# LayerNorm inverse roots moved to GpSimd, and the last two chunks of the last LayerNorm reordered

## Chip, core and metric

The kernel runs on one core of one Trainium2 chip. The metric is the device time of one execution in microseconds (us), the median of three runs. TensorE (PE) multiplies, VectorE (DVE), ScalarE (ACT) and GpSimd (POOL) do the element-wise work, and SyncE (SP) issues most of the transfers. DVE and ACT can read the matmul accumulators (PSUM, tiles `mm` and `ax`); POOL is only used on SBUF tiles here.

## The reference

One decoder layer over 1024 prompt tokens and 32 sample tokens, width 1024. What matters here are its three LayerNorms over the width:

```python
def layer_norm(x, g, b):
    mu = mean(x); var = mean((x - mu) ** 2)
    return (x - mu) * rsqrt(var + 1e-5) * g + b

h = layer_norm(ALPHA * x + 0.5 * swiglu(x, f1...), ln1_g, ln1_b)     # LN1
...  # z = h @ w_in, attention, gated MLP branch, mix
h = layer_norm(ALPHA * h + mix, ln2_g, ln2_b)                         # LN2
y = layer_norm(ALPHA * h + 0.5 * swiglu(h, f2...), ln3_g, ln3_b)      # LN3, the output
```

## The kernel before

Data lie transposed: features over the 128 partitions, the 1056 tokens along the free axis, in four chunks of 264 tokens (`C = 264`, `NC = 4`). A chunk of the residual stream is two tiles `Y[0]`, `Y[1]` of 128 x 4 x 264, four feature blocks each (`KH = 4`). Every LayerNorm is done chunk by chunk while TensorE goes on with the blocks of the next chunk:

- `block` (L925 in the two feed-forward networks, L1711 before LN2) adds a matmul result to `Y`; `square_step` squares it on ACT (L594) and sums the squares on DVE (L598, and L585 to L591 for the last blocks). `center` subtracts the mean (L549 on TensorE, L555 on DVE).
- `norm(c, i, mode)` is a generator, one per chunk `c` and LayerNorm `i`. It sums the squares over the partitions by a matmul with a column of ones (L607, result 128 x 3 in PSUM), takes the inverse root of variance plus epsilon on that 128 x 3 tile (names `X`), spreads the root to all partitions by a matmul with the identity (L621, result 128 x 264 in PSUM), multiplies `Y` by it on DVE (L632, one instruction of 128 x 1056 for each half `j`), applies gain and bias on ACT (L640; in the last chunk half of them on DVE, L637), and stores (L646 in LN3).
- The root has two forms before: `rsqrt` (L664 to L668: a Sqrt on ACT, which needs its own activation table, then a reciprocal and a Newton step of three instructions on DVE) and `rsqrt_dve` (L655 to L660: an integer first guess and three Newton steps, 11 DVE instructions).

The order of the work is set in two steps. The code emits the steps of the generators between matmul blocks (`tick`; `HOP` says how many steps a root may take before its spreading matmul is emitted), and a list scheduler then places each instruction in its engine's queue; work marked urgent (`high_priority`) goes ahead. Each engine then runs its own queue strictly in order, and waits at an instruction whose operands are not ready. What the chunks `NC - 2` and `NC - 1` (the last but one and the last, called chunk 2 and chunk 3 below; the first are chunk 0 and chunk 1) do in LN3 is the end of the program. Weights are split on the way in and out of LN1 and LN2 into a rounded part (ACT, L253) and a rest (DVE, L254), so ACT and DVE are busy there with other work too. An L338 or L348 on DVE prepares sums of normalized chunks for the next matrix product.

Of the kernel before, what the change touches and what calls it, by code (L numbers as in the profile page):

```python
# [14 lines left out]
I32 = mybir.dt.int32  # L15
AF = mybir.ActivationFunctionType
ALU = mybir.AluOpType
# [4 lines left out]
P = 128  # L22
# [5 lines left out]
C = 264  # L28
NC = NT // C
KH = KB // 2  # L30
# [14 lines left out]
EPL = EPS / ALPHA**2  # L45
# [11 lines left out]
URGENT = 300  # L57
# [7 lines left out]
HOP = (4, 1, 4)  # L65
WARM = 2
MAGIC = float(0x5F3759DF)
# [16 lines left out]
class Trunk:  # L84
# [392 lines left out]
    def spill_sums(self, i, a, b):  # L477

        nc = self.nc
        x11, x12, x21, x22 = a[:, :, 0], a[:, :, 1], b[:, :, 0], b[:, :, 1]  # L480

        def out(p, t):
            hi = self.M([P, 2, C], F32R)
            self.split(hi, t.bitcast(F32R), t)
            dst = self.sums[i, ORDER.index(p)]
            nc.sync.dma_start(dst[:, 0], hi.bitcast(F32))
            nc.sync.dma_start(dst[:, 1], t)
            return self.pause(GAP)

        sub = lambda t, u, v: nc.vector.tensor_tensor(t, u, v, op=ALU.subtract)  # L490
        t1, t2 = (self.M([P, 2, C]) for _ in range(2))
        sub(t1, x12, x11)
        yield from out(1, x11)
        sub(t2, x22, t1)
        yield from out(5, t1)
        sub(x12, x22, x12)
        yield from out(7, x12)
        t4 = self.M([P, 2, C])
        sub(t4, x21, t2)
        yield from out(6, t2)  # L500
        yield from out(3, x22)
        yield from out(4, t4)
        yield from out(2, x21)
# [96 lines left out]
    def norm(self, c, i, mode, Y, s):  # L600
        nc = self.nc
        offs = (0, P, C - P)
        if mode != "out" or c < NC - 1:
            nc.vector.tensor_tensor(s[:, 0], s[:, 0], s[:, 1], op=ALU.add)
        pv = self.ax_tile()[:, :3]
        for j, o in enumerate(offs):
            nc.tensor.matmul(pv[:, j : j + 1], s[:, 0, o : o + P], self.ones[:, 0:1], start=True, stop=True)  # L607
        rt = self.X([P, 2, 3], "rs")
        r, t = rt[:, 0], rt[:, 1]
        if c == NC - 1 and i == 1 or c == NC - 2 and mode == "out":  # L610
            self.rsqrt_dve(r, t, self.X([P, 3], "rx", 1), pv, EPL)
        else:
            self.rsqrt(r, t, pv, EPL)
        if i == 1 and c == NC - 2:
            nc.scalar.activation(self.X([P, 2], "warm", 1)[:, :1], r[:, :1], AF.Silu)
        for _ in range(HOP[i]):
            yield
        pb = self.ax_tile()[:, :C]
        for j, o in enumerate(offs):
            lo = 0 if j < 2 else 2 * P - o  # L620
            nc.tensor.matmul(  # L621
                pb[:, o + lo : o + P], r[:, j : j + 1].to_broadcast([P, P]), self.ident[:, lo:], start=True, stop=True
            )
        yield
        while mode == "out" and c == NC - 2 and NC - 1 not in self.lns:
            yield
        if mode != "out":
            A = self.normed[c]
        cast = None
        for j in range(2):  # L630
            y = Y[j]
            nc.vector.tensor_tensor(y, y, pb.unsqueeze(1).to_broadcast([P, KH, C]), op=ALU.mult)  # L632
            for m in range(KH):
                n = KH * j + m
                g, b = self.vec(2 * i, n), self.vec(2 * i + 1, n)
                if c == NC - 1 and m % 2:
                    nc.vector.tensor_scalar(y[:, m], y[:, m], g, b, op0=ALU.mult, op1=ALU.add)  # L637
                else:
                    with self.tc.issue_after(cast) if cast else ExitStack():
                        nc.scalar.activation(y[:, m], y[:, m], AF.Identity, bias=b, scale=g)  # L640
            yield
            if mode == "out":
                parts = 2 if c == NC - 1 else 1
                for m in range(parts):
                    e = slice(m * KH // parts, (m + 1) * KH // parts)
                    nc.sync.dma_start(self.a["yo"][c, j][:, e], y[:, e])  # L646
            else:
                cast = self.split(*A[j], y)[0]
                nc.sync.dma_start(self.hD[i][c, j], y)
            yield  # L650

    def rsqrt_dve(self, r, t, x, v, eps):
        nc = self.nc
        tt = nc.vector.scalar_tensor_tensor
        nc.vector.tensor_scalar(x, v, eps, None, op0=ALU.add)  # L655
        nc.vector.tensor_scalar(r.bitcast(I32), x.bitcast(I32), -0.5, MAGIC, op0=ALU.mult, op1=ALU.add)
        for _ in range(3):
            nc.vector.tensor_tensor(t, x, r, op=ALU.mult)
            tt(t, t, -0.5, r, op0=ALU.mult, op1=ALU.mult)
            self.chain = tt(r, t, 1.5, r, op0=ALU.add, op1=ALU.mult).ins  # L660

    def rsqrt(self, r, t, v, eps):
        tt = self.nc.vector.scalar_tensor_tensor
        self.nc.scalar.activation(r, v, AF.Sqrt, bias=self.eps[eps])  # L664
        self.nc.vector.reciprocal(r, r)
        tt(t, v, eps, r, op0=ALU.add, op1=ALU.mult)
        tt(t, t, -0.5, r, op0=ALU.mult, op1=ALU.mult)
        self.chain = tt(r, t, 1.5, r, op0=ALU.add, op1=ALU.mult).ins  # L668
# [156 lines left out]
    def out(self, w2, i, mode, ready, between, load):  # L825
        nc = self.nc
# [44 lines left out]
        for g in range(NG):  # L871
            for np in range(KB // 2):
                final = g == NG - 1 and np == KB // 2 - 1
# [53 lines left out]
        for c in range(NC):  # L927
# [15 lines left out]
                self.tick(STEPS["out"])  # L943
            self.start_ln(c, i, mode)
        if mode == "out":
            self.drain()

    def tables(self):
# [960 lines left out]
```

## Time and profile before

| | |
|---|---|
| runs | 2154.41 us median of 3 (2153.32 to 2157.72) |
| profiled execution | 2154.51 us, of which the span of the profile is 2152.5 us |
| granted TensorE clock | 0.994 of full speed |
| busy | PE 2122.6 us, DVE 1549.5 us, ACT 889.4 us, POOL 317.1 us |
| roots, four in each LayerNorm | 10 with `rsqrt` (L664), 2 with `rsqrt_dve` (chunk 3 of LN2, chunk 2 of LN3) |
| table loads of ACT for L664 | 4, of 1283 ns each |
| LN1, LN2, LN3 in the trace | first L607 at 679.2, 1401.4 and 2105.0 us |

"Busy" is summed over instructions of one engine; an engine is idle when the instruction at the head of its queue waits. A row of the timeline gives start, duration, engine, line, operation, tiles, and in brackets the idle time before it and who ended it. Times are us from the start of the span.

### The profile page before, as it was taken

What the parts mean: (1) busy time and instruction counts of PE and PEld (TensorE: products, weight loads), DVE (VectorE), ACT (ScalarE), POOL (GpSimd) and SP (SyncE); (2) the same over time, 40 slices, a digit from 0 to 9 for tenths busy, and PEclk for the clock granted to TensorE, in tenths of its full rate; (3) what the DMA queues carried; (4) which work ended last, traced back from release to release, by engine and by line L of the source; (5) the groups of instructions that cost most, each with busy time, mean ns of one, the idle gap of its engine ahead of it and who ended that gap; (6) DMA issues with size and microseconds to landing.
All of it is one profiled execution on the core that took longest, in us unless ns stands there. A gap on an engine that the chain in (4) does not pass through costs nothing.

```text
span 2152.5 us, 43254 instructions
## 1 busy us (share of the span) xinstructions
PE 2122.6 (99%) x17307; PEld 2085.6 (97%) x17307; DVE 1549.5 (72%) x2727; ACT 889.4 (41%) x1680; POOL 317.1 (15%) x249
## 2 busy tenths in 40 slices
PE   9999999999999999999999999999999999999997
PEld 8999999999999999999988889999999999999997
DVE  8877767747789834777767758787667777657887
ACT  5444444422124634333476544164444444421224
POOL 0432322200000011323000000000323323100000
PEclk9999999999999999999999999999999999999998
DMA  4444555598885335676865765423454554596852
GB/s 155 145 140 170 183 166 168 189 338 315 327 325 176 130 103 177 201 231 198 296 211 187 223 190 177 154 110 110 144 174 156 183 173 153 194 408 267 311 186 81
DMA packets 168377, 426.51 MB, mean 198 GB/s; under 512 B 24352, under 2 KB 59792, under 8 KB 165488
## 3 DMA queue, kind: packets, MB, share of 16 engines
q1 hardware_dynamic: 167744, 423.21, 56.4%
q8 instruction: 135, 2.21, 0.4%
q10 hardware_dynamic: 432, 0.54, 0.1%
q14 instruction: 66, 0.54, 0.1%
HBM read 304.31 MB, written 165.57 MB: 218 GB/s over the span
## 4 chain that ended last, share of the span: by engine, by line
PE 89%; DVE 4%; DMA 4%; POOL 1%; issue 1%; ACT 0%; SPq 0%; ACTq 0%; DVEq 0%; POOLq 0%
PE ax L242 46%; PE mm L242 39%; DMA R<-wz 1%; PE ax L1206 1%; DMA M<-kv 1%; DMA S<-cD 1%; PE ax L1255 1%; PE ax L1232 1%; DVE W L254 1%; DMA S<-hD 0%; DVE S L632 0%; POOL Q L392 0%; POOL Q L387 0%; DVE S L254 0%; PE ax L621 0%
## 5 line engine op out<-in xcount | busy, mean ns | idle before, releaser
L242 PE MATMUL mm<-S,W 128*128 128x264 f32 x5400 | 713.6, 287 | 8.0 <-ACT S L253 2.3
L242 PE MATMUL ax<-S,W 128*128 128x264 f32 x5400 | 708.6, 285 | 1.3 <-ACT S L1034 1.1
L242 PEld LDWEIGHTS mm<-S,W 128*128 128x128 f32 x5400 | 677.1, 189 | 21.0 <-issue 7.0
L242 PEld LDWEIGHTS ax<-S,W 128*128 128x128 f32 x5400 | 678.5, 189 | 4.0 <-ACT S L1034 2.4
L242 PE MATMUL ax<-S,S 128*128 128x264 f32 x3240 | 475.9, 284 | 1.0 <-ACT S L1034 0.5
L242 PEld LDWEIGHTS ax<-S,S 128*128 128x128 f32 x3240 | 427.7, 188 | 1.7 <-DVE S L1043 0.9
L242 PE MATMUL mm<-S,S 128*128 128x264 f32 x2280 | 359.4, 286 | 2.6 <-DVE S L925 2.6
L242 PEld LDWEIGHTS mm<-S,S 128*128 128x128 f32 x2280 | 311.0, 189 | 3.9 <-issue 2.9
L253 ACT CAST W<-R 128x256 fp32r<-128x256 f32 (+2 forms) x175 | 130.6, 764 | 307.5 <-PE mm L242 139.9
L386 POOL TENSOR_TENSOR Q<-R 128x512 f32<-128x512 f32 x49 | 68.1, 1390 | 800.8 <-DMA R<-w13a 198.2
L254 DVE TENSOR_TENSOR W<-R,W 128x256 fp32r<-128x256 f32 (+2 forms) x175 | 154.6, 887 | 23.3 <-ACT W L253 21.7
L253 ACT CAST W<-Q 128x1024 fp32r<-128x1024 f32 (+1 forms) x78 | 76.8, 984 | 217.2 <-POOL Q L387 88.1
L820 DVE SCALAR_TENSOR_TENSOR S<-ax,S 128x264 f32<-128x264 f32 x240 | 99.7, 429 | 66.1 <-PE ax L242 65.7
L462 DVE TENSOR_TENSOR S<-ax,M 128x264 f32<-128x264 f32 x82 | 32.6, 433 | 144.7 <-PE ax L242 144.7
L254 DVE TENSOR_TENSOR S<-Q,S 128x1024 fp32r<-128x1024 f32 (+1 forms) x78 | 113.6, 1456 | 5.5 <-ACT S L253 5.4
L110 POOL CAST S<-ones 128x1 fp32r<-128x1 f32 x36 | 12.5, 355 | 675.7 <-PE ax L242 226.0
L254 DVE TENSOR_TENSOR W<-Q,W 128x1024 fp32r<-128x1024 f32 (+1 forms) x78 | 90.6, 1161 | 29.6 <-ACT W L253 29.6
L253 ACT CAST S<-Q 128x1024 fp32r<-128x1024 f32 (+1 forms) x78 | 76.7, 984 | 68.4 <-PE ax L242 49.8
L254 DVE TENSOR_TENSOR S<-S,M 128x528 fp32r<-128x528 f32 x72 | 84.6, 1175 | 2.5 <-ACT M L253 0.7
L253 ACT CAST S<-R 128x512 fp32r<-128x512 f32 (+1 forms) x62 | 42.0, 677 | 98.9 <-DMA sumsA<-S 40.6
L387 POOL TENSOR_TENSOR Q<-Q,R 128x512 f32<-128x512 f32 x49 | 81.0, 1653 | 2.7
L394 POOL TENSOR_TENSOR Q<-R,Q 128x512 f32<-128x512 f32 x49 | 79.7, 1627 | 1.2
(209 smaller groups left out, 2042.5 us busy)
## 6 DMA issues: line engine op xcount, KB each, us to landing
ws<-st SPq DMA_DIRECT2D x144, 256.0 KB
S<-sumsA SPq DMA_DIRECT2D x63, 528.0 KB
S<-sumsB SPq DMA_DIRECT2D x63, 528.0 KB
M<-kv SPq DMA_DIRECT2D x96, 256.0 KB
sumsA<-M SPq DMA_DIRECT2D x90, 264.0 KB
sumsB<-M SPq DMA_DIRECT2D x90, 264.0 KB
R<-w13b SPq DMA_DIRECT2D x44, 512.0 KB
R<-w13a SPq DMA_DIRECT2D x42, 512.0 KB
```

The lines of the kernel that those rows point to most:

```text
L110: self.nc.gpsimd.tensor_copy(t[:, 0, :1] if len(shape) == 3 else t[:, :1], self.ones[:, :1])
L242: mm = lambda a, b, s, e: nc.tensor.matmul(o, a[:, cc], b, start=s, stop=e, skip_group_check=True)
L253: a = self.nc.scalar.copy(hi, src)
L254: b = self.nc.vector.tensor_tensor(lo, src, hi.bitcast(F32), op=ALU.subtract)
L386: tt(s12[:, lo], cd[:, lo], cd[:, hi], op=ALU.add)
L387: tt(s12[:, hi], s12[:, lo], ab[:, lo], op=ALU.subtract)
L394: tt(s34[:, hi], ab[:, hi], s12[:, hi], op=ALU.subtract)
L462: go(one, 5, False, lambda x: tt(h[:, x, 1], one[x], p7[:, x], op=ALU.add))
L820: nc.vector.scalar_tensor_tensor(y(x, r, e), bank[x], HALF, y(x, r, e), op0=ALU.mult, op1=ALU.add)
L1206: m = nc.tensor.matmul(pS[h][:, r, :nk], q[e, i * P : (i + 1) * P], k[e, k0 : k0 + nk], start=True, stop=True)
L1232: nc.tensor.transpose(pT[r][:, h, o], s[:, r, h, o], self.ident)
L1255: nc.tensor.matmul(pv[0][e, (i % 4) * P : (i % 4 + 1) * P], V[:, i - (nb - 1) + b, e], sT[:, r, h, b * P : b * P + P], start=b == 0, stop= ...
```

## The change

Eleven of the twelve roots (all four of LN1, all four of LN2 and three of the four of LN3) now use the new `rsqrt_pool`: an ACT instruction copies variance plus epsilon from PSUM to SBUF (Identity, no table of its own), and 13 POOL instructions on 128 x 3 elements follow, each reading what the one before wrote. Only chunk 3 of LN3 keeps `rsqrt` with its Sqrt. In LN3 chunk 2 four things are new: a small Sqrt on ACT that loads the table ahead of time (L617 in the new numbering), one step instead of four between the root and its spreading matmul, the scaling L632 in quarters (128 x 528), of which the last two are placed behind the root of chunk 3, and that root's first step is emitted urgently before the rest. The last of the four transfers of chunk 3 is issued by ACT's queue instead of SP's.

```diff
-        if c == NC - 1 and i == 1 or c == NC - 2 and mode == "out":
-            self.rsqrt_dve(r, t, self.X([P, 3], "rx", 1), pv, EPL)
+        if c == NC - 1 and mode == "out":
+            self.rsqrt(r, t, pv, EPL)
         else:
-            self.rsqrt(r, t, pv, EPL)
+            self.rsqrt_pool(r, t, self.X([P, 3], "rx"), pv, EPL)
         if i == 1 and c == NC - 2:
             nc.scalar.activation(self.X([P, 2], "warm", 1)[:, :1], r[:, :1], AF.Silu)
-        for _ in range(HOP[i]):
+        if mode == "out" and c == NC - 2:
+            nc.scalar.activation(self.X([P, 2], "warm", 1)[:, :1], self.eps[EPL], AF.Sqrt)
+        for _ in range(1 if mode == "out" and c == NC - 2 else HOP[i]):
             yield
...
-            nc.vector.tensor_tensor(y, y, pb.unsqueeze(1).to_broadcast([P, KH, C]), op=ALU.mult)
+            parts = 2 if mode == "out" and c == NC - 2 else 1
+            for x in range(0, KH, KH // parts):
+                e = y[:, x : x + KH // parts]
+                with self.chained() if parts > 1 and j else ExitStack():
+                    nc.vector.tensor_tensor(e, e, pb.unsqueeze(1).to_broadcast([P, KH // parts, C]), op=ALU.mult)
...
-                    nc.sync.dma_start(self.a["yo"][c, j][:, e], y[:, e])
+                    queue = nc.scalar if j and m else nc.sync
+                    queue.dma_start(self.a["yo"][c, j][:, e], y[:, e])
...
+    def rsqrt_pool(self, r, t, x, v, eps):
+        tt, ts = self.nc.gpsimd.tensor_tensor, self.nc.gpsimd.tensor_scalar
+        self.nc.scalar.activation(x, v, AF.Identity, bias=self.eps[eps])
+        ts(r.bitcast(I32), x.bitcast(I32), -0.5, MAGIC, op0=ALU.mult, op1=ALU.add)
+        for _ in range(3):
+            tt(t, x, r, op=ALU.mult)
+            tt(t, t, r, op=ALU.mult)
+            ts(t, t, -0.5, 1.5, op0=ALU.mult, op1=ALU.add)
+            tt(r, r, t, op=ALU.mult)
...
         if mode == "out":
+            final = self.bg.pop()
+            with self.tc.high_priority(offset=URGENT):
+                next(final)
+            self.bg.append(final)
             self.drain()
```

Over the whole program POOL gets 143 instructions more, DVE 56 fewer; ACT loses five table loads (four for L664 and one behind them) and gets one (L617), two more copies, and one transfer to issue. Outside the three LayerNorms all queues are the same.

TensorE's queue in LN1, at the spreading matmul of chunk 0 (`ax_8169` before, `ax_8179` after; `mm_8329` and `mm_8267` are block results, twelve L242 each; L549 is the mean of chunk 3). Before:

```order
L242 MATMUL mm_8329<-S_7823,W_7869 128x264
L242 MATMUL mm_8329<-S_7822,W_7870 128x264
L621 MATMUL ax_8169<-ident,X_8126 128x128 x2
L621 MATMUL ax_8169<-ident,X_8126 128x8
L549 MATMUL ax_8178<-M_8134,ones 128x264
```

After:

```order
L242 MATMUL mm_8267<-S_7823,S_7994 128x264
L242 MATMUL mm_8267<-S_7822,S_7995 128x264
L623 MATMUL ax_8179<-ident,X_8126 128x128 x2
L623 MATMUL ax_8179<-ident,X_8126 128x8
L549 MATMUL ax_8188<-M_8144,ones 128x264
```

The spreading matmul (L621, now L623) has moved two blocks ahead: 36 L242 stand between chunk 0's L607 and it, where there were 60.

DVE's queue at the end of the program, from the last sum of squares of chunk 3 (L591) on; `ax_25672` and `ax_25739` are chunk 2's spread root, `ax_25771` and `ax_25857` chunk 3's variance, `ax_25781` and `ax_25881` chunk 3's spread root. Before:

```order
L591 TENSOR_TENSOR M_25621<-M_25621,M_25756 128x264
L660 SCALAR_TENSOR_TENSOR X_25628<-X_25628 128x3
L632 TENSOR_TENSOR S_22648<-S_22648,ax_25672 128x1056
L632 TENSOR_TENSOR S_22874<-S_22874,ax_25672 128x1056
L665 RECIPROCAL X_25775<-X_25775 128x3
L666 SCALAR_TENSOR_TENSOR X_25775<-ax_25771,X_25775 128x3
L667 SCALAR_TENSOR_TENSOR X_25775<-X_25775 128x3
L668 SCALAR_TENSOR_TENSOR X_25775<-X_25775 128x3
L632 TENSOR_TENSOR S_22768<-S_22768,ax_25781 128x1056
```

After:

```order
L591 TENSOR_TENSOR M_25714<-M_25714,M_25854 128x264
L638 TENSOR_TENSOR S_22721<-S_22721,ax_25739 128x528 x2
L682 RECIPROCAL X_25861<-X_25861 128x3
L683 SCALAR_TENSOR_TENSOR X_25861<-ax_25857,X_25861 128x3
L684 SCALAR_TENSOR_TENSOR X_25861<-X_25861 128x3
L685 SCALAR_TENSOR_TENSOR X_25861<-X_25861 128x3
L638 TENSOR_TENSOR S_22947<-S_22947,ax_25739 128x528 x2
L638 TENSOR_TENSOR S_22841<-S_22841,ax_25881 128x1056
```

Half of chunk 2's scaling (L632, now L638) has moved behind chunk 3's root.

ACT's queue at the same place. Before:

```order
L585 ACTIVATE M_25738<-S_22876 128x264
L664 ACTIVATE X_25775<-ax_25771,eps_165 128x3
L640 ACTIVATE S_22648<-S_22648,cols 128x264 x4
L640 ACTIVATE S_22874<-S_22874,cols 128x264 x4
L640 ACTIVATE S_22768<-S_22768,cols 128x264 x2
L640 ACTIVATE S_22876<-S_22876,cols 128x264 x2
```

After:

```order
L585 ACTIVATE M_25836<-S_22949 128x264
L646 ACTIVATE S_22721<-S_22721,cols 128x264 x2
L681 ACTIVATE X_25861<-ax_25857,eps_165 128x3
L646 ACTIVATE S_22721<-S_22721,cols 128x264 x2
L646 ACTIVATE S_22947<-S_22947,cols 128x264 x4
L646 ACTIVATE S_22841<-S_22841,cols 128x264 x2
L646 ACTIVATE S_22949<-S_22949,cols 128x264 x2
L653 DMA yo<-S_22949 128x528
```

The Sqrt of chunk 3 (L664, now L681) now stands behind two gain-and-bias instructions of chunk 2, and the last transfer stands at the end of this queue.

## The prediction

> **What bounds the kernel now.** I read the page's head first, then the waits of TensorE, then the timeline of the end and of each LayerNorm.
>
> ```profile
> span 2152.5 us, 43254 instructions
> PE 2122.6 (99%) x17307; PEld 2085.6 (97%) x17307; DVE 1549.5 (72%) x2727; ACT 889.4 (41%) x1680; POOL 317.1 (15%) x249
> ...
> PE mm L242 <- DVE S L925: 3.2, 4, 1.9
> PE ax L621 <- DVE X L668: 2.7, 1, 2.7
> ...
> PE ax L621 <- DVE X L660: 1.6, 1, 1.6
> ```
>
> TensorE is busy for 99% of the span. A wait row gives the total, how often, and the longest. The spreading matmul L621 waited for a root only twice, 2.7 and 1.6 us, and both times at the end of the program. So ten of the twelve roots are already hidden: there the change can only lose, and only if a root comes later than TensorE reaches L621. What it can win lies in the end, whose rows follow (start, duration, engine, line, operation, and in brackets the idle time before it).
>
> ```profile
> 2133.43 0.72 PE L607 MATMUL ax<-ones,M 128*128 128x1 f32 x6
> ...
> 2138.42 0.43 DVE L591 TENSOR_TENSOR M<-M,M 128x264 f32<-128x264 f32 x1
> 2138.77 0.15 DVE L660 SCALAR_TENSOR_TENSOR X<-X 128x3 f32<-128x3 f32 x1
> 2139.07 0.81 PE L621 MATMUL ax<-ident,X 128*128 128x128 f32 x6 [1.64 <-DVE X L660]
> 2139.73 0.81 PE L607 MATMUL ax<-ones,M 128*128 128x1 f32 x6
> 2139.91 2.42 DVE L632 TENSOR_TENSOR S<-S,ax 128x1056 f32<-128x1056 f32 x2 [0.99 <-PE ax L621]
> 2140.58 0.26 ACT L664 ACTIVATE X<-ax,eps 128x3 f32<-128x3 f32 x1 [3.47 <-PE ax L607]
> 2141.20 4.09 ACT L640 ACTIVATE S<-S,cols 128x264 f32<-128x264 f32 x8 [0.36 <-DVE S L632]
> 2142.25 0.17 DVE L665 RECIPROCAL X<-X 128x3 f32<-128x3 f32 x1
> 2143.22 1.42 PE L621 MATMUL ax<-ident,X 128*128 128x128 f32 x6 [2.69 <-DVE X L668]
> 2144.68 2.42 DVE L632 TENSOR_TENSOR S<-S,ax 128x1056 f32<-128x1056 f32 x2 [1.60 <-PE ax L621]
> 2147.02 1.39 DVE L637 TENSOR_SCALAR S<-S,cols 128x264 f32<-128x264 f32 x4
> 2148.89 0.40 SPq L646 DMA_DIRECT2D yo<-S  x1
> ...
> 2148.50:2149.00 0.50, 0.00 (x0) 0.00 (x0) 0.00 (x0) 0.00 (x0) 0.00 (x0) 0.50 1.03 397
> ```
>
> Chunk 3's Sqrt (L664) has its value by 2140.84, but DVE is in chunk 2's two L632 until 2142.33, and the reciprocal only starts at 2142.25. This 1.4 us lies on the path that ends the program: reciprocal, Newton step, L621, L632, gain and bias, transfer.
>
> **The price of a root on GpSimd.** The first row below is the list of line L110 (minimum, median and maximum in ns), the last but two its mean; the trace has no 128 x 3 arithmetic on POOL.
>
> ```profile
> L110 POOL CAST S<-ones x36: 178/184/1268, 597.3 to 2041.7; 128x1 fp32r<-128x1 f32 x36
> 1517.17 1.29 POOL L387 TENSOR_TENSOR Q<-Q,R 128x512 f32<-128x512 f32 x1
> 1518.55 1.29 POOL L394 TENSOR_TENSOR Q<-R,Q 128x512 f32<-128x512 f32 x1
> L110 POOL CAST S<-ones 128x1 fp32r<-128x1 f32 x36 | 12.5, 355 | 675.7 <-PE ax L242 226.0 <-DMA S<-sumsA 188.7 <-DVE S L1692 96.7
> ...
> 708.66 1.23 DVE L254 TENSOR_TENSOR S<-R,S 128x1024 fp32r<-128x1024 f32 x1 [1.25 <-PE mm L242]
> 708.81 1.12 POOL L110 CAST S<-ones 128x1 fp32r<-128x1 f32 x1 [54.62 <-PE mm L242]
> ```
>
> A tiny POOL instruction takes 0.184 us, and one that needs the result of the one before it (L394 reads what L387 wrote) starts 0.09 us after its end. I take 0.184 + 0.08 = 0.264 us for each of the 13 steps: 3.4 us undisturbed. From above, the mean of the casts, 0.355, gives 13 x 0.435 = 5.65 us. Between these ends I stay at the median and count the disturbance by itself: the cast of 708.81 took 1.12 instead of 0.18 us, and it ended 0.04 us after the DVE instruction with two SBUF operands (L254) that had begun 0.15 us before it. So a step that meets such a DVE instruction waits for its end. The 0.355 is the same effect, averaged over 36 places.
>
> [...]
>
> [...]
>
> **LN1 and LN2, where the spreading matmul has moved.** What counts for a root is how many L242 stand between its L607 and its spreading matmul. In the order of the changed kernel these are, for chunks 0 to 3: LN1 36, 51, 60, 51 (before 60, 67, 107, 42); LN2 51, 51, 65, 67 (before 30, 39, 42, 66); LN3 48, 67 for chunks 0 and 1 (before 55, 45). The tight one is chunk 0 of LN1:
>
> ```profile
> 679.20 0.72 PE L607 MATMUL ax<-ones,M 128*128 128x1 f32 x6
> 679.42 1.05 ACT L253 CAST W<-R 128x1024 fp32r<-128x1024 f32 x1 [2.49 <-DMA R<-wzp]
> 680.16 4.62 PE L242 MATMUL mm<-S,S 128*128 128x264 f32 x36 [0.23 <-DVE S L925]
> 680.49 1.28 ACT L664 ACT_TABLE_LOAD   x1
> 681.05 1.22 DVE L254 TENSOR_TENSOR W<-R,W 128x1024 fp32r<-128x1024 f32 x1
> 681.78 0.26 ACT L664 ACTIVATE X<-ax,eps 128x3 f32<-128x3 f32 x1
> 682.26 0.41 DVE L546 TENSOR_TENSOR M<-M,S 128x264 f32<-128x264 f32 x1
> 682.70 0.71 DVE L598 TENSOR_TENSOR M<-M,M 128x528 f32<-128x528 f32 x1
> 684.28 0.71 DVE L598 TENSOR_TENSOR M<-M,M 128x528 f32<-128x528 f32 x1
> 684.62 3.09 PE L242 MATMUL mm<-S,W 128*128 128x264 f32 x24
> 687.54 0.73 PE L621 MATMUL ax<-ident,X 128*128 128x128 f32 x6
> ```
>
> The first 36 L242 take 684.62 - 680.16 = 4.46 us, 0.124 us each. With only these ahead of it TensorE is at the spreading matmul at 684.62 instead of 687.54. The root: the table load is gone, so the Identity runs right behind the cast, to about 680.75; 3.4 us of POOL steps end at 684.2 if nothing meets them. The four DVE instructions with two SBUF inputs in that stretch are 1.22 + 0.41 + 0.71 + 0.71 = 3.05 us; a POOL step that waits loses the rest of one, and I take two thirds, 2.0 us. The root is ready at 686.2, TensorE waits 1.6 us (0 to 3). Behind the root on DVE stand the two scalings (2.42 us, as in the row of 2139.91), and behind them the evictions of the next blocks, which come late too: another 0 to 2.4, I take 0.7. Together +2.3 us.
>
> Chunk 2 of LN2 has a second way to be late: the warm Silu on ACT (L615) reads the root, so ACT stands at it until POOL's chain is done, with the rounding of a weight behind it in its queue.
>
> ```profile
> 1437.74 0.73 PE L607 MATMUL ax<-ones,M 128*128 128x1 f32 x6
> 1438.33 5.39 PE L242 MATMUL mm<-S,W 128*128 128x264 f32 x42
> 1440.91 1.25 DVE L338 TENSOR_TENSOR S<-S,S 128x1056 f32<-128x1056 f32 x1
> 1442.28 1.22 DVE L254 TENSOR_TENSOR W<-R,W 128x1024 fp32r<-128x1024 f32 x1
> ```
>
> 65 matmuls are 8.1 us, so TensorE is there at about 1446.5. In these 8 us some seven DVE instructions like L338 and L254 (1.25 and 1.22 us) run, so a chain of 3.4 us that waits for two to five of them takes 6 to 9.6 us and is late by 0 to 1.9; I take 1.0. Chunk 3 of LN2 (67 matmuls, 8.3 us, but with POOL in place of DVE) 0 to 1.5, I take 0.4. The four roots with 48 or 51 matmuls in LN1 and LN2 and chunk 0 of LN3 have 6.0 to 6.3 us. They need some 0.5 us to the end of the Identity plus a chain which, with waits as in chunk 0 of LN1, is 5.4 us: 5.9. They are in time by 0.1 to 0.4, and I add 0.3 us for them together. The removed table loads (1.28 us each) and the 56 DVE instructions removed are worth nothing by themselves: no wait of TensorE there names ACT's root, and both engines have idle time to spare (41% and 72% busy). LN1 to LN3 without the end: +4.0 us, from 0 to +9.
>
> **The end.** Chunk 2's L607 now stands 11 matmuls earlier (37 behind it, 26 before), 1.4 us, so it ends at about 2132.8, with the Identity at 2133.1 and the chain of 3.4 us plus 0.7 to 1.1 of waits done at 2137.2 to 2137.6. Its L621 can then run once the last L242 is done, at some 2137.7, and not at 2139.07. Chunk 3's L607 hangs on L591, which ended at 2138.85 with chunk 2's root steps on DVE (L660 and those before it) between; without them it can be a little earlier, but I take the same time. DVE then does two quarters of chunk 2 (1.21 us) before the L607 of chunk 3 is answered. ACT does two gain-and-bias instructions (4.09 / 8 = 0.51 each) and the Sqrt (0.26) behind them, ending about 2140.8, as before. The reciprocal, which waited until 2142.25 for the second L632, can start at 2140.8: -1.45 us. The other two quarters (1.21 us) fit into DVE's wait of 1.60 us for the last L621, and everything from there on keeps its lengths. If POOL's chain for chunk 2 is 2 us longer, the quarters begin later and nothing is won; so -1.8 to 0, I take -1.45.
>
> The last transfer on ACT's queue is worth 0: the issue on SP at 2148.89 is the last of a row of issues, and in the window from 2148.50 on the DMA engines are 100% busy (1.03) at 397 GB/s. Transfers wait for the DMA engines there, not for a queue. The small Sqrt for the table costs nothing, ACT idled 3.47 us ahead of L664.
>
> **The sum.** The profiled execution took 2154.51 us (span 2152.5 and 2.0 around it), 0.1 above the median of 2154.41. 2154.5 + 4.0 - 1.45 = 2157.0. What a measurement of this kernel can tell from no change is 0.2%, 4.3 us, so bounds 2150.1 and 2158.7: this is no measurable change, on the slow side.
>
> **Rivals.**
> - All chains in LN1 and LN2 stay hidden, and only the end shows: 2154.5 - 1.45 = 2153.0. For it: the margins of the 60 to 67 matmuls, and that a POOL step which starts first is not stopped. Against it: 36 matmuls in LN1 chunk 0 leave 0.4 us over an undisturbed chain. Chance 0.23.
> - Slower: POOL loses to DVE more often than I count. The place is the roots with 48 to 51 matmuls, and it decides from 0.3 us more per chain than my 5.4. With one more wait of 1.2 us (L254) in each chain five roots are late by 0.9 (4.5 us), chunk 0 of LN1 by 2.3 + 1.2, chunk 2 of LN2 by 1.0 + 1.2, chunk 3 by 0.4, and the end keeps only 0.3 of its gain: 2154.5 + 10.6 - 0.3 = 2164.8. With every step at the mean of 0.355 us plus waits it is up to 2170. For it: the 1.12 us cast, DVE 72% busy. Against it: the median of 36 casts is 184 ns, so most met nothing. Chance 0.25.
> - The end does nothing: chunk 2's root is late there by the 2 us above. Then 2154.5 + 4.0 = 2158.5. Chance 0.05. For it: chunk 3's sums of squares (L598) run on DVE in just that stretch.
>
> **How the numbers follow.** The forecast case has the rest, 0.45, with a range of 2154 to 2161, and some 0.02 is left for a gain that I don't see: TensorE's idle time apart from the start and the end is some 3 us, so that a gain of 4.3 us would need all of it and the end. The range goes from the first rival (2152 with 1 us of slack) to the beginning of the second's prices: 2152 to 2164 leaves out about half of the second rival and the 0.02. Slower by over 0.2%: all of the second rival, a fifth of the forecast case (0.08) and no more; the rest is the same.
>
> **What would show it.** In the profile after: a wait of TensorE at L623 for POOL's last step, of about 1.6 us in chunk 0 of LN1, and of about 1 us around chunk 2 of LN2; the POOL steps L674 to L677 with a median near 0.18 us and a mean of 0.3 or so; at the end the reciprocal (L682) right behind the Sqrt, with no L638 between, about 1.4 us nearer to the last L242 than before; the DMA engines still full after the last issue. I am wrong if a 128 x 3 step on POOL takes 0.3 us and more without any DVE instruction beside it, if TensorE waits at L623 in five or more places, or if no such wait is there at all.

## The result, and the profile after

The changed kernel took 2168.06 us (median of 6 runs, 2166.65 to 2169.14), the kernel before 2156.26 us (6 runs, 2153.32 to 2159.71). The ratio is 1.0058, with a 95% interval of 1.0048 to 1.0068: slower by 0.6%, or 11.8 us between the medians. Forecast were 2157.0 us and "no measurable change", with a range up to 2164. The rival with GpSimd losing to DVE (2164.8, and up to 2170) came nearer. All medians and ratios in this document are over fast runs; the one slow run on record, of 5298.12 us in kernel e3 below, is left out.

The page's head and the waits of TensorE, after:

```profile
span 2166.2 us, 43330 instructions
PE 2126.1 (98%) x17307; PEld 2088.2 (96%) x17307; DVE 1540.2 (71%) x2671; ACT 883.2 (41%) x1679; POOL 370.3 (17%) x392
```

```profile
PE ax L623 <- POOL X L677: 7.7, 6, 2.8
PE ax L242 <- ACT S L1055: 4.1, 4, 2.4
PE mm L242 <- DVE S L942: 3.6, 4, 1.9
PE ax L623 <- ACT S L646: 2.4, 1, 2.4
```

TensorE now waits six times for POOL at the spreading matmul, 7.7 us in all, where it had waited for no root outside the end. That is little more than half of the 13.7 us between the two spans. To see where the rest went, the start of each L242 was set against that of the same L242 (counted from the first) before. The lag of the changed kernel is -0.5 us ahead of LN1 and 2.7 us at its end, moves between 0.2 and 5.5 us in the stages between (where nothing was changed), grows from 5.3 to 15.1 us within LN2 (between 1443 and 1467 us of the kernel before), and stays at 14.1 to 16.6 us in LN3. So 9.8 us were lost in 24 us of LN2. Its timeline, after, for chunk 2 and then chunk 3:

```profile
1443.28 0.72 PE L607 MATMUL ax<-ones,M 128*128 128x1 f32 x6
...
1443.87 8.13 PE L242 MATMUL mm<-S,W 128*128 128x264 f32 x65
1443.98 1.03 ACT L253 CAST W<-R 128x1024 fp32r<-128x1024 f32 x1
...
1444.92 0.42 ACT L594 ACTIVATE M<-S 128x264 f32<-128x264 f32 x1
1445.24 0.24 ACT L671 ACTIVATE X<-ax,eps 128x3 f32<-128x3 f32 x1
...
1445.64 2.50 POOL L110 CAST S<-ones 128x1 fp32r<-128x1 f32 x3 [9.46 <-DMA ws<-st]
...
1448.02 1.25 DVE L254 TENSOR_TENSOR S<-S,S 128x1056 fp32r<-128x1056 f32 x1
...
1448.23 1.10 POOL L672 TENSOR_SCALAR X<-X 128x3 int32<-128x3 int32 x1
...
1454.60 0.19 POOL L677 TENSOR_TENSOR X<-X 128x3 f32<-128x3 f32 x1
...
1454.84 1.45 PE L623 MATMUL ax<-ident,X 128*128 128x128 f32 x6 [2.84 <-POOL X L677]
...
1456.14 10.45 PE L242 MATMUL mm<-S,W 128*128 128x264 f32 x65
...
1467.01 8.33 PE L242 MATMUL mm<-S,W 128*128 128x264 f32 x67
...
1467.54 1.01 POOL L672 TENSOR_SCALAR X<-X 128x3 int32<-128x3 int32 x1 [12.75 <-ACT X L671]
...
1468.75 1.26 DVE L254 TENSOR_TENSOR S<-S,S 128x1056 fp32r<-128x1056 f32 x1
...
1468.91 4.69 POOL L675 TENSOR_TENSOR X<-X 128x3 f32<-128x3 f32 x1
1469.92 0.69 DVE L394 TENSOR_TENSOR Q<-R,Q 128x512 f32<-128x512 f32 x1
...
1470.52 2.43 DVE L348 TENSOR_TENSOR S<-S,S 128x1056 fp32r<-128x1056 f32 x2
1472.86 0.69 DVE L254 TENSOR_TENSOR S<-R,S 128x512 fp32r<-128x512 f32 x1
...
1477.43 0.83 PE L623 MATMUL ax<-ident,X 128*128 128x128 f32 x6 [2.09 <-POOL X L677]
```

Two things are to be seen. The roots are late by 2.84 and 2.09 us: 4.9 us. POOL's steps end with the DVE instructions beside them: the step of 1448.23 takes 1.10 us instead of 0.20 and ends 0.06 us after the L254 of 1448.02; L675 in chunk 3 takes 4.69 us, ends 0.05 us after the L254 of 1472.86, and five DVE instructions passed it. And after the first wait 65 L242 take 10.45 us, where the 65 ahead of it took 8.13; six L623 take 1.45 us, at the second wait 0.83. The windows of the changed kernel show why (the value after the last bracket is the granted TensorE clock, then DMA share and GB/s):

```profile
1454.80:1461.20 6.40, 6.36 (x29) 6.36 (x30) 5.21 (x5) 3.36 (x7) 0.00 (x0) 0.50 0.47 164
1461.20:1467.00 5.80, 5.80 (x50) 5.80 (x50) 5.80 (x9) 5.77 (x10) 0.00 (x0) 0.99 0.38 148
1478.40:1481.80 3.40, 3.40 (x18) 3.40 (x18) 2.33 (x2) 0.00 (x0) 0.00 (x0) 0.50 0.00 0
1481.80:1485.00 3.20, 3.20 (x28) 3.20 (x28) 1.11 (x4) 1.38 (x3) 0.00 (x0) 1.00 0.03 5
```

Behind each wait TensorE ran at half the granted clock, 6.8 us after the first and 3.4 us after the second by windows of a quarter of a microsecond, and so lost another 3.4 + 1.7 = 5.1 us. Waits and clock together are 10.0 us, against the 9.8 of the lag (the first stretch at half clock began 0.3 us before its wait ended, so this much is counted in part twice). The waits cost twice what their rows say.

The end became shorter, by less than forecast:

```profile
2153.31 0.83 PE L623 MATMUL ax<-ident,X 128*128 128x128 f32 x6 [1.07 <-POOL X L677]
...
2154.00 0.81 PE L607 MATMUL ax<-ones,M 128*128 128x1 f32 x6
2154.18 1.32 DVE L638 TENSOR_TENSOR S<-S,ax 128x528 f32<-128x528 f32 x2 [0.51 <-PE ax L623]
2154.93 1.10 ACT L646 ACTIVATE S<-S,cols 128x264 f32<-128x264 f32 x2 [3.06 <-DVE S L638]
2155.94 0.24 ACT L681 ACTIVATE X<-ax,eps 128x3 f32<-128x3 f32 x1
...
2156.21 0.18 DVE L682 RECIPROCAL X<-X 128x3 f32<-128x3 f32 x1 [0.71 <-ACT X L681]
...
2157.19 1.00 PE L623 MATMUL ax<-ident,X 128*128 128x128 f32 x6 [2.38 <-ACT S L646]
```

The last L242 ends at 2152.24; from there to the end of the span it is 13.98 us, 15.10 before: 1.1 us won.

### The profile page after: what moved, and what is told of

It is laid out like the page before. It is cut to its first block, busy times and chain, and to the rows that moved or that the text cites. A ratio compares the mean times of both kernels' runs of the same rounds, so it can differ in the third digit from the quotient of the medians.

```text
span 2166.2 us, 43330 instructions
## 1 busy us (share of the span) xinstructions
PE 2126.1 (98%) x17307; PEld 2088.2 (96%) x17307; DVE 1540.2 (71%) x2671; ACT 883.2 (41%) x1679; POOL 370.3 (17%) x392
## 3 DMA queue, kind: packets, MB, share of 16 engines
q8 instruction: 135, 2.21, 0.4%
## 4 chain that ended last, share of the span: by engine, by line
PE 86%; DMA 5%; DVE 4%; POOL 2%; issue 1%; ACT 1%; SPq 0%; ACTq 0%; DVEq 0%; POOLq 0%
PE ax L242 47%; PE mm L242 36%; PE ax L1227 1%; DMA S<-zD 1%; DMA M<-kv 1%; DMA S<-cD 1%; PE ax L1276 1%; PE ax L1253 1%; DVE W L254 1%; POOL X L675 1%; DMA R<-wz 1%; DMA S<-hD 0%; DVE S L638 0%; PE ax L623 0%; PE mm L1572 0%
## 5 line engine op out<-in xcount | busy, mean ns | idle before, releaser
L242 PE MATMUL mm<-S,W 128*128 128x264 f32 x5400 | 717.1, 288 | 8.3 <-DVE S L1606 1.9
L242 PE MATMUL ax<-S,W 128*128 128x264 f32 x5400 | 706.8, 285 | 3.1 <-ACT S L1055 2.9
L242 PEld LDWEIGHTS mm<-S,W 128*128 128x128 f32 x5400 | 680.7, 190 | 21.4 <-issue 7.0
L242 PEld LDWEIGHTS ax<-S,W 128*128 128x128 f32 x5400 | 676.9, 188 | 5.7 <-ACT S L1055 4.0
L242 PE MATMUL ax<-S,S 128*128 128x264 f32 x3240 | 476.2, 285 | 1.8 <-ACT S L1055 1.2
L242 PEld LDWEIGHTS ax<-S,S 128*128 128x128 f32 x3240 | 428.0, 188 | 2.5 <-ACT S L1055 1.4
L242 PE MATMUL mm<-S,S 128*128 128x264 f32 x2280 | 359.6, 286 | 2.1 <-DVE S L942 2.1
L242 PEld LDWEIGHTS mm<-S,S 128*128 128x128 f32 x2280 | 311.2, 189 | 3.4 <-issue 2.9
L253 ACT CAST W<-R 128x256 fp32r<-128x256 f32 (+2 forms) x175 | 130.6, 764 | 309.6 <-PE mm L242 139.5
L386 POOL TENSOR_TENSOR Q<-R 128x512 f32<-128x512 f32 x49 | 73.3, 1495 | 756.2 <-DMA R<-w13b 203.8
L254 DVE TENSOR_TENSOR W<-R,W 128x256 fp32r<-128x256 f32 (+2 forms) x175 | 159.7, 916 | 25.2 <-ACT W L253 23.6
L253 ACT CAST W<-Q 128x1024 fp32r<-128x1024 f32 (+1 forms) x78 | 76.8, 984 | 219.3 <-POOL Q L387 90.1
L254 DVE TENSOR_TENSOR W<-Q,W 128x1024 fp32r<-128x1024 f32 (+1 forms) x78 | 90.1, 1155 | 31.1 <-ACT W L253 30.9
L254 DVE TENSOR_TENSOR S<-Q,S 128x1024 fp32r<-128x1024 f32 (+1 forms) x78 | 107.8, 1382 | 5.5 <-ACT S L253 5.5
L253 ACT CAST S<-Q 128x1024 fp32r<-128x1024 f32 (+1 forms) x78 | 76.7, 983 | 68.1 <-PE ax L242 49.9
L254 DVE TENSOR_TENSOR S<-S,M 128x528 fp32r<-128x528 f32 x72 | 83.6, 1161 | 3.8 <-ACT M L253 2.2
L253 ACT CAST S<-R 128x512 fp32r<-128x512 f32 (+1 forms) x62 | 42.0, 677 | 99.0 <-DMA sumsA<-S 41.4
```

What stands on the lines that cost most here:

```text
L242: mm = lambda a, b, s, e: nc.tensor.matmul(o, a[:, cc], b, start=s, stop=e, skip_group_check=True)
L253: a = self.nc.scalar.copy(hi, src)
L254: b = self.nc.vector.tensor_tensor(lo, src, hi.bitcast(F32), op=ALU.subtract)
L386: tt(s12[:, lo], cd[:, lo], cd[:, hi], op=ALU.add)
```

## The experiments

Theory A: the loss is in LN2, where two roots come late because POOL's steps wait for DVE, and each wait also halves the clock for a while. Theory B: GpSimd and DVE slow each other in general, each root costs about the same. All kernels below start from the kernel before or from the changed one, and each ratio is against runs of the kernel before on the same chip. e7, e8, e10 and e11 ran once each, and only their rows are used.

**1 to 4: one part at a time.** The condition under which a root is made on POOL:

```diff
 # e1, from the changed kernel; where it doesn't hold, the forms of before
+        if i != 1 and not (c == NC - 1 and mode == "out"):
+            self.rsqrt_pool(r, t, self.X([P, 3], "rx"), pv, EPL)
 # e2, from the kernel before
+        if i == 1:
 # e3, from the kernel before
+        if i == 0:
 # e4, from the changed kernel
+        if c == NC - 2 and mode == "out":
```

> The changed kernel, with the four roots of LN2 as before (Sqrt on ACT for chunks 0 to 2, the DVE form for chunk 3); LN1, LN3 and the end stay changed. Theory A (the loss sits in LN2, where TensorE stood 2.84 and 2.09 us at the spreading matmuls of chunks 2 and 3 and then ran for some 6.5 and 3.3 us at half the granted clock): 9.8 us of the loss go, 2168.1 - 9.8 = 2158.3, about 0.1% above before; no stretch of clock 0.50 in LN2. Theory B (each root on GpSimd costs about the same, 12.9 us over eleven roots, by DVE and GpSimd disturbing each other): four roots give back 4.7 us, 2163.4.

> The kernel before, with only the four roots of LN2 on GpSimd. Theory A: before + 9.8 us, about 2166, with both waits at the spreading matmuls of chunks 2 and 3 and clock 0.50 behind each. Theory B: before + 4.7 us, about 2161.

> The kernel before, with only the four roots of LN1 on GpSimd. Theory A: a wait of about 1.2 us at chunk 0's spreading matmul, 0.4 at chunk 2's, no half clock: before + 2 to 3 us, about 2158.8. Theory B: before + 4.7 us, about 2161.

> The kernel before, with only what the change does in LN3's chunks 2 and 3 (chunk 2's root on GpSimd, its table load, its quarters, the urgent first step of chunk 3, the last transfer on ACT's queue); all other roots as before. Theory A: before - 1.1 us, about 2155.1 (ratio 0.9995), since in the trace of the changed kernel the 15.07 us from the last L242 to the end have become 13.95. Theory B: the one root on GpSimd costs 1.2 us more than that, the end stays at 2156.3.

| kernel | median us | before, same chip | ratio | 95% interval |
|---|---|---|---|---|
| e1, all but LN2 | 2156.85 | 2155.31 | 1.0011 | 1.0001 to 1.0021 |
| e2, LN2 only | 2164.21 | 2155.31 | 1.0045 | 1.0032 to 1.0058 |
| e3, LN1 only | 2158.33 | 2155.31 | 1.0013 | 1.0002 to 1.0024 |
| e4, the end only | 2155.59 | 2155.31 | 0.9996 | 0.9988 to 1.0005 |

By their ratios LN2 alone costs 9.7 us, LN1 2.8, and the end wins 0.9 and is not told apart from nothing. e1 and e2 came out as theory A has them. The intervals of e3 and e4 hold what either theory gave, so these two alone don't decide; but theory B falls, as LN1 with as many roots costs under a third of LN2, and their intervals (0.4 to 5.2 and 6.9 to 12.5 us) don't touch. In e4 the stretch from the last L242 to the end is 14.52 us, not the 13.95 expected: between chunk 2's L607 and its spreading matmul stand 26 L242 there, as in the kernel before, where the changed kernel has 37, and that matmul begins 0.45 us later (table below). In e2 the two waits stand in LN2 again:

```profile
1449.20 0.83 PE L623 MATMUL ax<-ident,X 128*128 128x128 f32 x6 [2.81 <-POOL X L672]
...
1471.69 1.24 PE L623 MATMUL ax<-ident,X 128*128 128x128 f32 x6 [4.94 <-POOL X L672]
```

This time they are 2.81 and 4.94 us, with 3.4 us of half clock (0.50, from 1471.96 to 1475.37) behind the second and none behind the first. The sum, 7.75 + 1.7 = 9.5 us, is nearly that of the changed kernel, though its parts are not. What was expected of e2, half clock behind both, was wrong.

**5: the casts ahead of chunk 2's root.**

```diff
-        self.normed[c] = [(self.held(...), self.held(...)) for _ in range(2)]        # cast on POOL
+        self.normed[c] = [tuple(self.held(..., self.nc.scalar.copy) for _ in range(2)) for _ in range(2)]
```

> The changed kernel, with the small holding casts of the normalized chunks (128x1, four per chunk) on ACT instead of POOL. In the trace of the changed kernel three of them stood ahead of chunk 2's root in LN2 and took 2.50 us (1445.64 to 1448.14), since DVE ran instructions with two SBUF operands. Theory A1 (queue ahead of the chain): the chain begins some 2.6 us earlier, the wait at chunk 2's spreading matmul falls from 2.84 to under 0.8 us, the clock is not halved there: 2168.1 - 2.4 - 3.4 = 2162.3. Theory A2 (DVE's instructions block the chain's steps anyway): the start moves, the end does not by more than 1 us: 2167 to 2168.

2165.67 us, ratio 1.0047 (1.0034 to 1.0059). The rows of this kernel:

```profile
1445.49 0.24 ACT L671 ACTIVATE X<-ax,eps 128x3 f32<-128x3 f32 x1
...
1445.82 0.20 POOL L672 TENSOR_SCALAR X<-X 128x3 int32<-128x3 int32 x1 [13.44 <-ACT X L671]
1445.96 1.22 DVE L254 TENSOR_TENSOR W<-R,W 128x1024 fp32r<-128x1024 f32 x1
1446.10 1.13 POOL L674 TENSOR_TENSOR X<-X,X 128x3 f32<-128x3 f32 x1
1447.10 1.25 DVE L338 TENSOR_TENSOR S<-S,S 128x1056 f32<-128x1056 f32 x1
1447.31 1.09 POOL L675 TENSOR_TENSOR X<-X 128x3 f32<-128x3 f32 x1
...
1454.27 0.83 PE L623 MATMUL ax<-ident,X 128*128 128x128 f32 x6 [2.13 <-POOL X L677]
```

The chain begins 0.1 us behind the Identity's end, where it was 2.75, and yet ends only 0.8 us sooner after it. The DVE instructions that had held up the casts now hold up the root's own steps: a step of 0.2 us becomes one of 1.1 that ends with the DVE instruction beside it. So A2 holds for the chain (8.4 us long, where casts and chain together had been 9.15), and the wait shrinks by 0.7 us; the queue ahead is not the main cause. The time lies between the two expectations and doesn't separate them: chunk 2 had 3.4 us less at half clock, but chunk 3 waited 3.26 us instead of 2.09, with 3.4 us more.

**6: ACT not held by the root.**

```diff
-            nc.scalar.activation(self.X([P, 2], "warm", 1)[:, :1], r[:, :1], AF.Silu)
+            nc.scalar.activation(self.X([P, 2], "warm", 1)[:, :1], self.eps[EPL], AF.Silu)
```

> The changed kernel, with LN2's warm Silu reading a constant instead of chunk 2's root, so that ACT does not stand at it for 5.5 us. Theory A (the chain on POOL alone decides, TensorE waits for it): 2168 +- 1.5, the wait at chunk 2's spreading matmul stays 2 to 4 us. Theory C (ACT's stand delays the weights that TensorE needs next): 2164 to 2166, with less DVE idle time in front of L254.

2163.95 us, ratio 1.0041 (1.0027 to 1.0054): below what theory A gave, and at C's edge, though the intervals of this and of the changed kernel overlap. The row of chunk 2 speaks against C all the same:

```profile
1453.96 1.45 PE L623 MATMUL ax<-ident,X 128*128 128x128 f32 x6 [5.24 <-POOL X L677]
```

Chunk 2's wait got longer, 5.24 us instead of 2.84, outside theory A's 2 to 4: with ACT free, DVE gets its next operands and has no idle time from 1443.28 to 1453.0, mostly in two-operand instructions, and nine of the 13 steps of POOL's chain are held up, to between 0.53 and 1.15 us instead of 0.20 (the chain goes from 1443.81 to 1453.91). In the changed kernel ACT's stand had starved DVE (idle for 3.46 us ahead of the L254 of 1455.99) and so let POOL finish. What is shorter in this trace is chunk 3, whose wait was gone, with a chain of 6.0 us instead of 9.8; the scheduler had moved DVE's work there (and the spreading matmul, to 62 L242 instead of 67), and which of it helped isn't separated.

**7: the disputed costs by themselves.** Behind the end of the kernel before, chains and bursts were appended:

```diff
+        for kind, n, k in (("alone", 0, 0), ("one", 512, 22), ("psum", 512, 22), ("two", 512, 22), ("two", 4 * C, 18)):
+            # a DVE stream of k instructions of that kind, and a chain of 13 POOL steps
+        for g in range(20):
+            # 110 to 138 matmuls in a row, then 2 to 11 DVE instructions before the next burst may start
```

> The kernel before, with a part appended behind its end (its time means nothing, only the rows of that part): five chains of 13 steps on POOL (128x3), alone and beside a stream of DVE instructions with one SBUF operand (128x512), with one SBUF and one PSUM operand (128x512), with two SBUF operands (128x512, then 128x1056); then 20 bursts of 110 to 138 matmuls with idle gaps of about 0.9 to 5 us between them. Theory A: alone, one operand and PSUM operand 3.6 us each (13 x 0.275); two SBUF operands: every step waits for one DVE instruction, 9 to 12 us at 0.68 us each, 16 to 20 us at 1.25 us each. Theory B (DVE and GpSimd slow each other in general): all four streams lengthen the chain alike, by a third or so. Clock: after what the eight profiles so far show, a gap of 1.9 us or more is followed by 3.4 us at half clock mostly, one of 1.2 us seldom; a rival says that only gaps over 3.4 us count.

The chains slid by one stream against the streams; by their rows they ran alone, beside one-operand DVE instructions (L1790, twice), beside SBUF and PSUM (L1792) and beside two SBUF operands (L1794), so no chain met the 128x1056 stream. One step (L1798) of each, by groups of the stretch:

```profile
L1798 POOL TENSOR_TENSOR X<-X 128x3 f32<-128x3 f32 x3 | 0.6, 193 | 0.2
...
L1798 POOL TENSOR_TENSOR X<-X 128x3 f32<-128x3 f32 x3 | 1.1, 380 | 0.2
L1790 DVE TENSOR_SCALAR S<-S 128x512 f32<-128x512 f32 x14 | 6.0, 427 | 0.4
...
L1798 POOL TENSOR_TENSOR X<-X 128x3 f32<-128x3 f32 x3 | 0.6, 193 | 0.2
...
L1798 POOL TENSOR_TENSOR X<-X 128x3 f32<-128x3 f32 x3 | 1.9, 646 | 0.2
```

In order: alone 193 ns (the chain 3.5 us), one operand 380 ns (5.8 us), PSUM operand 193 ns (3.5 us), two SBUF operands 646 ns (9.3 us). Beside the two SBUF streams each step lets one DVE instruction pass (0.43 us each with one operand, 0.69 with two). Theory A has the two-operand and the PSUM case right; it missed that DVE's single-operand instructions in SBUF hold POOL up too, and why they do, no trace here shows. B is wrong, since the PSUM stream changes nothing at the same DVE load (21 instructions in 15.13 us, with two SBUF operands in 15.21).

The bursts, rows of the same program (the idle gap in brackets; 131, 138 and 110 matmuls come with several gaps):

```profile
2278.07 16.43 PE L1809 MATMUL mm<-S,W 128*128 128x264 f32 x131 [1.52 <-DVE S L1813]
2296.35 16.83 PE L1809 MATMUL mm<-S,W 128*128 128x264 f32 x138 [1.85 <-DVE S L1813]
2315.37 13.83 PE L1809 MATMUL mm<-S,W 128*128 128x264 f32 x110 [2.19 <-DVE S L1813]
...
2369.53 17.93 PE L1809 MATMUL mm<-S,W 128*128 128x264 f32 x131 [3.19 <-DVE S L1813]
...
2481.62 18.78 PE L1809 MATMUL mm<-S,W 128*128 128x264 f32 x138 [1.85 <-DVE S L1813]
2502.58 15.03 PE L1809 MATMUL mm<-S,W 128*128 128x264 f32 x110 [2.19 <-DVE S L1813]
```

The same 138 matmuls behind the same gap of 1.85 us take 16.83 us once and 18.78 once, and 110 behind 2.19 us take 13.83 and 15.03. By windows of a quarter of a microsecond, half clock follows none of the four gaps of 1.19 and 1.52 us, five of the eight from 1.85 to 2.86, one of two at 3.19, and all three from 3.52 on. It lasts 3.41 us, or twice that behind 3.52. So in these bursts an idle gap of 1.85 to 3.19 us cost, in six places of ten, an estimated 1.7 us (half of 3.41) on top of its own length, and the rival with 3.4 us as the bound is wrong.

The traces also show what sets the same gaps apart. In the ten traces read in such windows (before, changed, e1 to e8) the changes of the granted clock lie whole multiples of 3.413 us apart, within 5 ns: on a grid (before, from 666.57 to 939.63 us, 80 steps), which lies elsewhere in each trace. In the bursts half clock came with the next step exactly when at least 1.85 us of one step were without a PE instruction (1.85, and 2.17 to 3.41), and never at 1.84 or less. The 2.19 us ahead of the 13.83 lay across two steps (1.81 and 0.38), those ahead of the 15.03 in one; the gap of 3.19 us that was followed by nothing lay across two as well (1.60 and 1.59). Behind the first 15 us of the kernel before and the changed one, all six steps at full clock with 1.85 us or more idle (1.90 to 2.51) were followed by half clock, and one (1.45) of the eleven with 1.0 to 1.7. The waits of LN2 agree: 2.51 us of the first and 2.09 of the second fell into one step in the changed kernel, 1.67 and 1.14 into two steps at the first wait of e2. So in these traces how much half clock a wait of 2 to 3 us brought hung on where it fell on the grid; that it differs between executions of one kernel follows, but is not shown, as each kernel was traced once.

**8: the last transfer's queue.**

```diff
-                    queue = nc.scalar if j and m else nc.sync
+                    queue = nc.sync
```

> The kernel of the run with the end alone, with the last transfer back on SP's queue. The prediction's worth of that edit is 0: from the end of the last gain-and-bias on DVE to the end of the span 4.2 us with either queue (within 0.1). Rival: ACT's queue saves up to one issue, 0.4 us.

From the end of the last DVE instruction (L645) to the end of the span it is 4.14 us on SP and 4.15 on ACT (e4): nothing, as forecast.

**9 to 11: the end, step by step.** In e9 and e10 LN1 and LN2 are as before and LN3 as changed; e9 also orders chunk 3's Sqrt. e11 is e4 without quarters.

```diff
 # e9
+        self.sqrt_ins = self.nc.scalar.activation(r, v, AF.Sqrt, bias=self.eps[eps]).ins
-                    with self.tc.issue_after(cast) if cast else ExitStack():
+                    with self.tc.issue_after(cast or self.sqrt_ins) if cast or mode == "out" and c == NC - 2 else ExitStack():
 # e11
-            parts = 2 if mode == "out" and c == NC - 2 else 1
+            parts = 1
```

> LN1 and LN2 as before; LN3 as in the changed kernel (chunks 0 to 2 on GpSimd, the quarters, the last transfer on ACT), and the Sqrt of chunk 3 ordered on ACT ahead of the gain-and-bias instructions of chunk 2. In the changed kernel this Sqrt stood behind two of them and began 1.94 us after L607 of chunk 3 (0.85 before). Theory A: the reciprocal begins 1.5 to 1.6 us after that L607 instead of 2.21 (the first two quarters on DVE end then), so the stretch from the last L242 to the end is 13.95 - 0.65 = 13.3 us (15.07 before); with no loss in LN1 and LN2 the time is 1.1 + 0.65 = 1.75 us below before, ratio 0.9992, which five rounds can hardly tell from 1. Rival: the quarters on DVE decide, the stretch stays at 13.9.

> The same without the order of the Sqrt: LN1 and LN2 as before, LN3 as in the changed kernel. From the last L242 to the end 13.95 us as in the changed kernel (within 0.2), no wait at LN3's first two spreading matmuls.

> The run with the end alone, with chunk 2's scaling in two halves as before, not in quarters. Theory A (the reciprocal waits for chunk 2's scaling on DVE): the reciprocal begins 2.5 us or more after L607 of chunk 3 (2.21 with quarters), the stretch from the last L242 to the end gets 0.3 to 0.5 us longer than with quarters (14.55). Rival: the Sqrt decides, no difference.

Times in us from the end of the last L242, of chunk 3's L607, its Sqrt and its reciprocal, the two spreading matmuls and the end of the span:

| kernel | chunk 2 spread | L607 | Sqrt | reciprocal | chunk 3 spread, to its end | end |
|---|---|---|---|---|---|---|
| before | 1.64 | 2.30 | 3.14 | 4.82 | 5.79 to 7.21 | 15.10 |
| changed | 1.07 | 1.76 | 3.69 | 3.96 | 4.95 to 5.94 | 13.98 |
| e4, the end only | 1.52 | 2.21 | 4.14 | 4.42 | 5.40 to 6.60 | 14.52 |
| e11, no quarters | 1.52 | 2.21 | 3.06 | 4.73 | 5.70 to 7.12 | 15.04 |
| e10, LN3 only | 1.07 | 1.76 | 3.69 | 3.96 | 4.94 to 6.36 | 14.27 |
| e9, Sqrt first | 1.07 | 1.76 | 2.66 | 3.18 | 4.15 to 5.16 | 13.35 |

e9 and e11 came out as theory A had them, or nearly: with the Sqrt ahead, the reciprocal begins 1.42 us after L607 (1.5 to 1.6 expected) and the stretch is 13.35; without quarters 2.52, and the stretch 0.5 us longer. In the changed kernel the Sqrt on ACT, not DVE, ends last. e10's 14.27 missed the 13.95 (within 0.2) by 0.1, and the table shows where: its last spreading matmul took 1.42 us, not 0.99, as the one of the kernel before did at a granted clock of 0.50. As a whole kernel e9 took 2153.82 us, before 2154.06: ratio 0.9997 (0.9988 to 1.0007). It is the best version found, and not told apart from the kernel before.

## Why the prediction was wrong, point by point

- **LN2, chunks 2 and 3** is the step that failed. Forecast: late by 1.0 (0 to 1.9) and 0.4 (0 to 1.5). Measured: 2.84 and 2.09 us, in e2 2.81 and 4.94. The mechanism was the one described (POOL steps that wait for DVE's two-operand instructions: 1.10 us instead of 0.20 beside the L254 of 1448.02), but two terms were mis-sized. In chunk 2 the chain itself took 6.56 us, within the 6 to 9.6 of the forecast; it began too late. The Identity stood in ACT's queue behind an L253 and an L594 and ended 1.48 us after L607 (0.5 was counted for the roots beside it), and POOL's queue held three casts ahead of the chain, which themselves waited for DVE: 2.75 us (run 5: worth 0.7 of the wait, as the steps then wait instead). In chunk 3 the chain took 9.84 us, where the ten other roots took 3.5 to 6.6: the forecast let each step wait for one DVE instruction, and L675 alone lost 4.5 us to five. TensorE waited for POOL at L623 in six places; five or more was the prediction's own sign of being wrong.
- **The clock** was no term at all, and so put at nothing without a reason. Half the loss of LN2, 5.1 us in the changed kernel, is time at half clock behind the waits. The evidence stood in the prediction's own rows: the L621 of 2143.22, behind a wait of 2.69 us, took 1.42 us for six matmuls, the one of 2139.07, behind 1.64 us, took 0.81. The prediction took no reading of the granted clock of that stretch; it is 0.50:

```profile
2143.22:2144.64 1.42, 1.42 (x6) 1.33 (x6) 0.00 (x0) 1.42 (x4) 0.00 (x0) 0.50 0.35 140
```

- **The price of a step** was right: 193 to 196 ns by the medians, forecast 0.184, and 3.5 us for an undisturbed chain, forecast 3.4. That a step lets one DVE instruction pass was right for most of those that met one, and wrong for the L675 of chunk 3, which let five pass.
- **LN1**: chunk 0's wait is 1.17 us, forecast 1.6, chunk 2's 0.35; the cost alone (e3) 2.8 us, forecast 2.3 for chunk 0 and a share of 0.3. Of the five roots with 48 or 51 L242 four don't wait for POOL in the changed kernel, and chunk 3 of LN1 does for 0.18 us. The second rival's place, just those roots, was therefore wrong, though its time was near: the roots of LN2 with the widest margins (65 and 67) were late, while one with 67 in LN3 was in time.
- **The end** was forecast at -1.45 and came out at -1.12. The reciprocal was to start where the Sqrt ends "as before"; but two gain-and-bias instructions (1.10 us for both) now stand ahead of the Sqrt, which begins 1.94 us after L607 instead of 0.84. The gain came instead from L607 (0.54 us sooner, since chunk 2's spreading matmul ahead of it is not held by DVE), 0.32 at the reciprocal, and 0.43 from a last spreading matmul of 0.99 us instead of 1.42, which is the clock again (0.50 all through it before, only from 2157.66 on after); behind it 0.15 were lost.
- The last queue and the removed table loads were worth nothing, as forecast. For the table loads (1.28 us each) no run stands apart; TensorE's waits of before, with all of them, and of e1, with some gone and some kept, name none of them.

By the runs with one part alone the sum is 9.7 + 2.8 - 0.9 = 11.6 us, the whole change 0.58% of 2156 = 12.5 us, in its interval 10.3 to 14.7. Chunks 0 and 1 of LN3, which stand in none of these runs, don't wait in the changed kernel.

## What to carry to other kernels

Here a chain of short dependent steps on GpSimd was as long as the SBUF-only DVE instructions beside it allowed (13 steps: 3.5 us alone, 5.8 and 9.3 us beside the SBUF streams of e7, up to 9.84 us in LN2): count those in the chain's window, at least one per step, before moving it there, and what already stands in POOL's queue. The two waits of LN2, 2.84 and 2.09 us, were followed here by 6.8 and 3.4 us at a granted clock of 0.50, so each cost an estimated 3.4 and 1.7 us on top of its length: price a wait with what may follow it, and read the granted clock behind a wait in the trace of before. There the six spreading matmuls of 1.42 us, against 0.81 for the six at full clock, were the sign. Behind a hidden step there was no gain here, only margin to lose.

## What the hardware showed unexpectedly

DVE instructions with a single SBUF operand (128x512, 0.43 us each) held up POOL's steps as two-operand ones did (380 and 646 against 193 ns), those with a PSUM operand not at all (193 ns). In the kernels a POOL step that met one mostly let one DVE instruction pass, but in three traces (the changed kernel, e2 and run 5) the same step of chunk 3 of LN2 took 4.69 us while five in a row passed, and in the changed kernel the first step of chunk 3 of LN1 took 2.68 us beside three L348; why, stays open. Half clock followed the same gap in one place and not in another (138 matmuls behind 1.85 us took 16.83 and 18.78 us): in the bursts it came where at least 1.85 us of one step of a grid of 3.413 us were idle, and lasted one step or two. The exceptions stay open: in four traces (before, e4, e5 and e8) 3.4 us of it also followed a step with 1.3 to 1.5 us idle between 915 and 940 us, and in e3 a step with 1.63 us idle at the end of the program.
